# A decoder trunk on one core: memory values by token, projections moved between stages, and rotary queries with channels on partitions

## The chip, the cores and the metric

The kernel runs on one core of a Trainium2 chip. The metric is device time in microseconds (us) of one execution; lower is better. Engine names are those of the profile: PE is the matrix engine (PEld its weight loads), DVE the vector engine, ACT the scalar engine, POOL the general engine, SP the engine that issues every DMA here.

## The reference

Two layers (DEPTH) of a trunk with S = 1024 tokens and D = 1024 channels. Each layer projects the stream `x` into four token mixers of 4 heads each (MLA with a rotary part, stick-breaking, forgetting attention "fox", attention over 256 memory rows), gates each, merges the four with sigmoid gates and normalizes. What the change touches:

```python
def _rope(x, cos, sin):
    x1, x2 = jnp.split(x, 2, axis=-1)
    return jnp.concatenate([x1 * cos - x2 * sin, x1 * sin + x2 * cos], axis=-1)
...
    q = (_rms_norm(c_q, q_norm) @ w_qb).reshape(b, s, MLA_HEADS, MLA_NOPE + MLA_ROPE)
    q_nope, q_pe = q[..., :MLA_NOPE], q[..., MLA_NOPE:]
    q_pe = _rope(q_pe, cos[:, :, None, :], sin[:, :, None, :])
...
    mk, mv = jnp.split(mem @ w_mem_kv, 2, axis=-1)
    y_mem = _memory_attention(mem_q..., mk, mv)
```

All of it is float32. The kernel splits every operand into a high and a low part (fp32r) and forms a product in three matmuls: high by high, high by low, low by high (`passes`).

## The kernel before

The work of a layer is a chain of stages. A stage is a `run(units, filler, total)`: the attention units of one mixer (a unit is one head and one group of 256 queries, `qg`), and between their steps `total` steps of a filler, mostly projections (`proj`: 8 blocks of weights, two halves of 512 tokens, 16 steps of three 128x512 matmuls). The stages are fox pair 0, fox pair 1, stick-breaking ("sb") pair 0, sb pair 1, memory, then the preparation of MLA and the MLA units with the merge (`mg`) as filler. A scheduler of the framework fixes the order on each engine when the kernel is built; each engine then runs its list in order.

Weights come through `Stream`: `wload` fetches 128x512 blocks by an SP DMA, and POOL splits each into `wh` (L163) and `wl` (L166). All DMAs stand in one SP list, in which a DMA that waits holds up those behind it.

**Memory.** `mem_prep` forms keys and values of a pair of heads channel by token (`mk`, `mv`, 24 matmuls of 256 columns each); `v_from_T` copies `mv` out to `mvT` and turns it on PE (L328, two transposes a pair) to get values token by channel.

**Rotary queries.** `mla_qpe(half)` forms `qpeT` (128 channels, 512 tokens), copies it to `qT`, turns it token by channel with 4 transposes (L1007, tile `qpe`), applies the rotation on DVE (`rope`, six operations), scales on POOL (L1013) and writes high and low parts into `t4` tiles (`qt`). `mla_qpT(half)` turns these back with 16 transposes (L1028, tile `qpT`) into one operand `qpe` per head (copied by ACT, L1030). The third matmul of an MLA score (`sc<-kpe,qpe`, L378) reads it.

**MLA start.** The merge of branch 2 runs beside the preparation. `load_y(1)` fetches four gated outputs `y` of sb back from `y_d` (SP, L1044), and `split_y` splits them (`ybh` on ACT, L157; `ybl` on DVE, L158) for the merge of branch 1. Each unit also needs `s2` (two 64 KB DMAs, L355 and L356), its query tile with halves swapped. In sb, `tri`-masked tiles `bt` pass POOL's `affine_select` (L425), and PE turns them (L464) before the value products.

Of the kernel before, what the change touches and what calls it, by code (L numbers as in the profile page):

```python
# [65 lines left out]
def decoder_trunk(ctx: ExitStack, tc: tile.TileContext, x, x_t, mem_t, positions, w_a, w_s, mla_q_norm, mla_w_qb,  # L66
# [55 lines left out]
    def f(ap):  # L122
        return ap.bitcast(F32)
# [72 lines left out]
    c_d = dp.tile([4, S], F32, name="c_d")  # L196

# [29 lines left out]
    def wload(n):  # L227

        raw = rp.tile([P, HALF], F32, tag="wr", name=nm("wr"))
        i = nc.sync.dma_start(raw, w_s[n])  # L230
        if n < 4:
            after(i, last_load[0])
        wh = hp.tile([P, HALF], F32R, tag="wh", name=nm("wh"))
        wl = hp.tile([P, HALF], F32R, tag="wl", name=nm("wl"))
        split_pool(raw, wh, wl)
        return [(wh[:, c:c + P], wl[:, c:c + P]) for c in range(0, HALF, P)]
# [24 lines left out]
    class Stream:  # L261
# [11 lines left out]
        def take(self, n, ahead=8):  # L273
# [3 lines left out]
            return r  # L277
# [360 lines left out]

    for layer in range(DEPTH):
# [170 lines left out]
        def mem_prep():  # L810
            for pair in range(2):
                w = st.take(KT)
                ps = PJ("mk")
                yield from passes(ps[:, :MEM], w, memT, KT)
                a = U("mk")
                ks = (a[:, 0:MEM], a[:, MEM:])
                for t, r0 in zip(ks, (0, 64)):
                    act.copy(t[r0:r0 + 64, :], ps[r0:r0 + 64, :MEM])
                for t, r0 in zip(ks, (0, 64)):
                    lo = 64 - r0  # L820
                    dve.tensor_tensor(t[lo:lo + 64, :], ps[r0:r0 + 64, :MEM], f(t[r0:r0 + 64, :]), ALU.subtract)
                mo[pair]["k"] = ks
                w = st.take(KT)
                ps = PJ("mv")
                yield from passes(ps[:, :MEM], w, memT, KT)
                t = TMP("mvT")
                act.copy(t[:, :MEM], ps[:, :MEM])
                mo[pair]["v"] = v_from_T([t], 2)
                yield
# [25 lines left out]
        run(fox_units(fox[0], 0), pair_qkv(fox[1], SC64), 49)  # L855
# [6 lines left out]
        run(units(sb[0], "sb"), pair_qkv(sb[1], SC64), 49)  # L862
# [4 lines left out]
        run(units(sb[1], "sb"), chain(cq_proj(), proj(evac_mr)), 58)  # L867
# [3 lines left out]
        drain(mem_prep())  # L871
# [3 lines left out]
        run(units(mo[0], "mem") + units(mo[1], "mem"), chain(proj(stack_pair(mo[1]["q"], SC64)), gate(2, 0), gate(2, 1), gate(1, 0), gate(1, 1)), 80)  # L875
# [79 lines left out]
        t4s = [[], []]  # L955
# [24 lines left out]
        def load_wq():  # L980
            for k in range(3):
# [4 lines left out]
                for c0, c1, d0 in ((0, 64, 0), (64, 96, 256)):  # L986
                    n = 4 * (c1 - c0)
                    hv, lv = (t[:, d0:d0 + n].rearrange("p (h c) -> p h c", h=4) for t in (h, l))
                    split_pool(sv[:, :, c0:c1], hv, lv)
# [8 lines left out]

        def mla_qpe(half):
            ps = PJ("qpeT")  # L1000
            yield from passes(ps, wsl(wq_h, wq_l, 3, 256), cqT[half], 3)
            qT = U("qT", F32)
            act.copy(qT, ps)
            yield QPE_STEPS
            ps = PT("qpe")
            for b in range(4):
                pe.transpose(ps[:, b * P:(b + 1) * P], qT[:, b * P:(b + 1) * P], ident)  # L1007
            src = ps.rearrange("p (b h c) -> p b h c", b=4, h=4)
            qr = U("qr", F32).rearrange("p (b h c) -> p b h c", b=4, h=4)
# [107 lines left out]
        def step(f):  # L1117
# [3 lines left out]
        main = chain(mla_ckvT(), mla_k(0), mla_k(1), step(load_wq), step(lambda: load_cq(1)), mla_v(0), mla_v(1),  # L1121
                     split_cq(1), step(lambda: load_cq(0)), mla_qpe(1), split_cq(0), mla_q(1), mla_qpe(0), mla_qpT(1), mla_q(0), mla_qpT(0))
# [25 lines left out]
        run(units(ml[0], "mla") + units(ml[1], "mla"), mg, 96 - MG_EARLY - MG_LATE, False)  # L1148
# [145 lines left out]
```

## Time and profile before

| | |
|---|---|
| median of 3 runs | 1573.8 us (1573.46 to 1574.72) |
| profiled execution, its own time | 1577.04 us |
| its span, first to last instruction | 1575.3 us |
| mean granted PE clock | 0.997 of full |
| PE busy | 1554.1 us (99%) |
| DVE, ACT, POOL busy | 1041.6, 724.2, 779.2 us |
| moved by DMA | 127.92 MB, mean 81 GB/s |

A busy PE is not PE at its peak: a matmul's record runs until its end, and the next one starts well before that. What an instruction costs on a full PE is the distance between the starts of neighbours.

### The profile page before, as it was taken

Reading aid. Unit: us, or ns where it says so; the run is one execution under the profiler, and the core shown is the slowest. Engines: PE = TensorE matmul, PEld = TensorE weight load, DVE = VectorE, ACT = ScalarE, POOL = GpSimd, SP = SyncE. Lnnn points to the kernel's source line nnn. Section 1 sums busy time; section 2 is a strip of 40 time slices with the busy share of each in tenths; the row PEclk is TensorE's granted clock in tenths of the full one; section 3 lists DMA queues with packets and bytes.
Section 4 is the critical chain, followed back from the end, with each engine's and each line's share of the span. In section 5 each row is a group of like instructions: output and inputs, shape, how many; then the busy total and the mean of one; then the engine's idle time right before and its main releaser. Section 6 shows DMA issues by size and latency. Waiting matters only on the chain.

```text
span 1575.3 us, 24794 instructions
## 1 busy us (share of the span) xinstructions
PE 1554.1 (99%) x8454; PEld 1331.2 (85%) x8454; DVE 1041.6 (66%) x2055; ACT 724.2 (46%) x1612; POOL 779.2 (49%) x951
## 2 busy tenths in 40 slices
PE   9999999999999999999999999999999999999997
PEld 8888888888888888888898888888988887888886
DVE  7455699844436788973853566997454377888738
ACT  4354566534434656440323556565344346564400
POOL 5666525765544344671336655357655442446600
PEclk9999999999999999999999999999999999999999
DMA  5321112142233211252313211122312232212413
GB/s 185 115 71 41 47 41 64 54 125 64 74 109 109 70 55 44 81 176 72 124 63 100 65 45 45 37 69 73 111 54 90 96 111 64 65 33 87 152 52 116
DMA packets 86061, 127.92 MB, mean 81 GB/s; under 512 B 13424, under 2 KB 38832, under 8 KB 85936
## 3 DMA queue, kind: packets, MB, share of 16 engines
q1 hardware_dynamic: 85936, 126.34, 25.6%
q8 instruction: 67, 1.10, 0.3%
q14 instruction: 58, 0.48, 0.1%
HBM read 89.57 MB, written 19.96 MB: 70 GB/s over the span
## 4 chain that ended last, share of the span: by engine, by line
PE 90%; DVE 3%; POOL 2%; issue 2%; ACT 2%; DMA 1%; SPq 0%; DVEq 0%; POOLq 0%; ACTq 0%
PE pj L254 13%; PE pj L255 13%; PE pj L256 13%; PE y L494 7%; PE pt L464 6%; PE po L255 4%; PE po L256 4%; PE po L254 4%; PE sc L375 3%; PE sc L376 3%; PE pb L254 3%; PE pb L255 3%; PE pb L256 3%; PE pg L254 1%; PE pg L256 1%
## 5 line engine op out<-in xcount | busy, mean ns | idle before, releaser
L254 PE MATMUL pj<-xTh,wh 128*128 128x512 f32 x832 | 331.2, 398 | 2.2 <-DVE mx L433 1.4
L256 PE MATMUL pj<-xTh,wl 128*128 128x512 f32 x832 | 326.5, 392 | 0.0
L255 PE MATMUL pj<-xTl,wh 128*128 128x512 f32 x832 | 325.8, 392 | 0.0
L166 POOL TENSOR_TENSOR wl<-wr,wh 128x512 fp32r<-128x512 f32 x168 | 226.4, 1349 | 9.9
L155 DVE TENSOR_TENSOR pl<-pt,ph 128x384 fp32r<-128x384 f32 (+1 forms) x272 | 170.3, 638 | 69.9 <-ACT ph L154 68.3
L163 POOL TENSOR_SCALAR wh<-wr 128x512 fp32r<-128x512 f32 x168 | 117.0, 697 | 193.6 <-PE pj L255 113.4
L154 ACT CAST ph<-pt 128x384 fp32r<-128x384 f32 (+1 forms) x272 | 147.8, 550 | 138.4 <-PE pt L464 134.1
L256 PEld LDWEIGHTS pj<-xTh,wl 128*128 128x128 f32 x832 | 156.3, 188 | 31.7
L254 PEld LDWEIGHTS pj<-xTh,wh 128*128 128x128 f32 x832 | 156.5, 188 | 28.8 <-DVE mx L433 1.8
L255 PEld LDWEIGHTS pj<-xTl,wh 128*128 128x128 f32 x832 | 156.6, 188 | 25.5
L445 POOL TENSOR_SCALAR p<-p,sm 128x896 f32<-128x896 f32 (+7 forms) x128 | 102.3, 801 | 149.0 <-DVE sm L444 147.2
L134 ACT ACTIVATE p<-p,mx 128x896 f32<-128x896 f32 (+7 forms) x128 | 99.5, 777 | 67.3 <-DVE mx L433 60.5
L494 PE MATMUL y<-pl,v 128*128 128x256 f32 (+1 forms) x544 | 124.6, 306 | 0.0
L134 ACT ACTIVATE mg<-pg 128x512 f32<-128x512 f32 x128 | 76.0, 597 | 83.8 <-PE pg L256 41.9
L494 PE MATMUL y<-ph,v 128*128 128x256 f32 (+1 forms) x544 | 112.2, 283 | 1.8 <-ACT ph L154 1.6
L464 PE MATMUL pt<-ident_r,p 128*128 128x128 f32 x704 | 110.9, 273 | 0.2
L494 PEld LDWEIGHTS y<-ph,v 128*128 128x128 f32 x544 | 93.4, 189 | 13.8 <-ACT ph L154 1.8
L254 PE MATMUL pb<-ybh,wh 128*128 128x512 f32 x256 | 102.8, 401 | 0.9 <-DVE mg L1090 0.6
L438 DVE TENSOR_TENSOR_SCAN kt<-kt,unseen 128x896 f32<-128x896 f32 (+3 forms) x64 | 96.3, 1516 | 10.1 <-ACT kt L134 9.8
L255 PE MATMUL pb<-ybl,wh 128*128 128x512 f32 x256 | 100.6, 393 | 0.0
L256 PE MATMUL pb<-ybh,wl 128*128 128x512 f32 x256 | 100.4, 392 | 0.0
L464 PEld LDWEIGHTS pt<-ident_r,p 128*128 128x128 f32 x704 | 85.1, 140 | 13.8 <-issue 0.5
(273 smaller groups left out, 3555.9 us busy)
## 6 DMA issues: line engine op xcount, KB each, us to landing
wr<-in_w_s_dram SPq DMA_DIRECT2D x168, 256.0 KB, 2.6
s<-opA SPq DMA_DIRECT2D x128, 64.0 KB, 2.0
s<-opB SPq DMA_DIRECT2D x128, 64.0 KB, 2.0
wr<-in_w_out_dram SPq DMA_DIRECT2D x32, 256.0 KB, 2.7
xr<-in_x_t_dram SPq DMA_DIRECT2D x16, 256.0 KB, 5.3
ckb<-c_d SPq DMA_DIRECT2D x8, 512.0 KB, 3.9
y_d<-y SPq DMA_DIRECT2D x16, 256.0 KB, 2.0
y<-y_d SPq DMA_DIRECT2D x16, 256.0 KB, 3.6
```

Of the source, the lines that this page charges most:

```text
L134: i = act.activation(*args, **kw)
L154: act.copy(h, src)
L155: return dve.tensor_tensor(l, src, f(h), ALU.subtract)
L163: i = pool.tensor_scalar(h, src, 1.0, 1.0, ALU.mult, ALU.mult)
L166: pool.tensor_tensor(l, src, f(h), ALU.subtract)
L254: pe.matmul(ps, ah, bh, start=k == 0, stop=False)
L255: pe.matmul(ps, ah, bl, start=False, stop=False)
L256: pe.matmul(ps, al, bh, start=False, stop=k == nk - 1)
L438: dve.tensor_tensor_scan(kt[:, ::-1], kt[:, ::-1], unseen[:, S - w:][:, ::-1], 1.0, ALU.mult, ALU.max)
L445: pool.tensor_scalar(p, p, sm, 1.0, ALU.mult, ALU.mult)
L464: pe.transpose(pt[:, c:c + P], self.p[i][:, b * P:(b + 1) * P], ident)
L494: pe.matmul(u.y[:, q0 * P:256], u.op["v"][b][:, u.head, :], src[:, s * 256 + q0 * P:s * 256 + 256], start=j == 0 and n == 0, stop=j == n_c ...
```

## The change

**Memory.** The values are formed token by channel: the memory tokens are the stationary operand and 256 columns of weights the moving one (`take_two`), 48 matmuls of 256 columns as before, without `mvT` and its transposes. `mem_k(1)` moves into the filler of the memory stage.

**Moved projections.** The first of the three `cq` projections moves from sb pair 1 to sb pair 0 (total 49 to 65), `gate(2, 0)` from the memory stage into sb pair 1 (58 to 64); the memory stage goes from 80 to 72 steps. The weight blocks are put in the same order.

**Rotary queries.** In layer 0, `rotary_tables` turns cosine and sine once into tables with channels on partitions (16 transposes, beside fox pair 0) and stores them (`tab_d`, 4 DMAs of 256 KB). `load_tabs` fetches a 512 KB table for each half. `mla_qpe` now turns the queries where they stand: three DVE multiplies that read `qpeT` in PSUM and one DVE add, a copy of the high part on ACT, the low part on POOL. Four DMAs of 256 KB store the parts twice each (`qr_d`), and four of 256 KB fetch one operand `qpe` per head. `mla_qpT` is gone. `mla_q(0)` now stands ahead of `mla_qpe(0)`, and the second and third MLA units are swapped.

```diff
-            return r
+            return [(wh[:, c:c + P], wl[:, c:c + P]) for wh, wl, c in r]
+        def take_two(self):
+            self.pull(2)
+            (wh, wl, c), self.blocks = self.blocks[0], self.blocks[2:]
+            self.pull()
+            return wh[:, c:c + 2 * P], wl[:, c:c + 2 * P]
...
+    def rotary_tables():
+        for n, src in enumerate((cosT, sinT)):
+            for half in range(2):
+                rows = U("rows", F32)
+                pool.tensor_scalar(rows.rearrange("p (b r c) -> p b r c", b=4, r=8),
+                                   src[:, 4 * half:4 * half + 4, :].unsqueeze(2).broadcast_to((P, 4, 8, 16)), 1.0, 1.0, ALU.mult, ALU.mult)
+                ps = PT("tab")
+                for b in range(4):
+                    pe.transpose(ps[:, b * P:(b + 1) * P], rows[:, b * P:(b + 1) * P], ident)
+                t = TMP("tab")
+                if n == 0:
+                    act.activation(t, ps, AF.Copy, scale=SC96)
+                else:
+                    act.activation(t[0:64, :], ps[0:64, :], AF.Copy, scale=SC96)
+                    act.activation(t[64:128, :], ps[64:128, :], AF.Copy, scale=-SC96)
+                nc.sync.dma_start(tab_d[half][:, n, :], t)
+                yield
     for layer in range(DEPTH):
...
                 yield
             mem_raws.clear()
-        def mem_prep():
+        def mem_k(pair):
+            w = st.take(KT)
+            ps = PJ("mk")
+            yield from passes(ps[:, :MEM], w, memT, KT)
+            a = U("mk")
+            ks = (a[:, 0:MEM], a[:, MEM:])
+            for t, r0 in zip(ks, (0, 64)):
+                act.copy(t[r0:r0 + 64, :], ps[r0:r0 + 64, :MEM])
+            for t, r0 in zip(ks, (0, 64)):
+                lo = 64 - r0
+                dve.tensor_tensor(t[lo:lo + 64, :], ps[r0:r0 + 64, :MEM], f(t[r0:r0 + 64, :]), ALU.subtract)
+            mo[pair]["k"] = ks
+        def mem_v():
+            pss = [PJ("mv")[:, :256] for _ in range(2)]
+            for k in range(KT):
+                wh, wl = st.take_two()
+                for b in range(2):
+                    th, tl = (m[:, b * P:(b + 1) * P] for m in memT[k])
+                    pe.matmul(pss[b], th, wh, start=k == 0, stop=False)
+                    pe.matmul(pss[b], tl, wh, start=False, stop=False)
+                    pe.matmul(pss[b], th, wl, start=False, stop=k == KT - 1)
+                yield
             for pair in range(2):
-                w = st.take(KT)
-                ps = PJ("mk")
-                yield from passes(ps[:, :MEM], w, memT, KT)
-                a = U("mk")
-                ks = (a[:, 0:MEM], a[:, MEM:])
-                for t, r0 in zip(ks, (0, 64)):
-                    act.copy(t[r0:r0 + 64, :], ps[r0:r0 + 64, :MEM])
-                for t, r0 in zip(ks, (0, 64)):
-                    lo = 64 - r0
-                    dve.tensor_tensor(t[lo:lo + 64, :], ps[r0:r0 + 64, :MEM], f(t[r0:r0 + 64, :]), ALU.subtract)
-                mo[pair]["k"] = ks
-                w = st.take(KT)
-                ps = PJ("mv")
-                yield from passes(ps[:, :MEM], w, memT, KT)
-                t = TMP("mvT")
-                act.copy(t[:, :MEM], ps[:, :MEM])
-                mo[pair]["v"] = v_from_T([t], 2)
-                yield
+                mo[pair]["v"] = []
+            for ps in pss:
+                t = U("v").rearrange("p (h c) -> p h c", h=4)
+                src = ps.rearrange("p (h c) -> p h c", h=4)
+                act.copy(t[:, :, 0:64], src)
+                dve.tensor_tensor(t[:, :, 64:128], src, f(t[:, :, 0:64]), ALU.subtract)
+                for pair in range(2):
+                    mo[pair]["v"].append(t[:, 2 * pair:2 * pair + 2])
+            yield
         def gate_evac(n, pair):
...
         drain(pair_qkv(fox[0], SC64))
         fox[0].update(new_op())
         ys[(2, 0)] = fox[0]["y"]
-        run(fox_units(fox[0], 0), pair_qkv(fox[1], SC64), 49)
+        tables = () if layer else rotary_tables()
+        run(fox_units(fox[0], 0), chain(pair_qkv(fox[1], SC64), tables), 49 if layer else 53)
         fox[1].update(new_op())
         ys[(2, 1)] = fox[1]["y"]
         run(fox_units(fox[1], 1), pair_qkv(sb[0], SC64), 49)
         sb[0].update(new_op())
         ys[(1, 0)] = sb[0]["y"]
         table("sigmoid_and_others")
-        run(units(sb[0], "sb"), pair_qkv(sb[1], SC64), 49)
+        cqs = cq_proj()
+        run(units(sb[0], "sb"), chain(pair_qkv(sb[1], SC64), itertools.islice(cqs, 2 * KT)), 65)
         sb[1].update(new_op())
         ys[(1, 1)] = sb[1]["y"]
         for pair in range(2):
             mo[pair]["q"] = two_halves()
-        run(units(sb[1], "sb"), chain(cq_proj(), proj(evac_mr)), 58)
+        run(units(sb[1], "sb"), chain(cqs, proj(evac_mr), gate(2, 0)), 64)
         table("natural_log_exp_and_others")
         load_mem()
         drain(weave(proj(stack_pair(mo[0]["q"], SC64)), chain(split_mem(), cq_norm()), 1))
-        drain(mem_prep())
+        drain(mem_k(0))
+        drain(mem_v())
         table("exp_and_others")
         for pair in range(2):
             mo[pair].update(new_op())
-        run(units(mo[0], "mem") + units(mo[1], "mem"), chain(proj(stack_pair(mo[1]["q"], SC64)), gate(2, 0), gate(2, 1), gate(1, 0), gate(1, 1)), 80)
+        run(units(mo[0], "mem") + units(mo[1], "mem"), chain(proj(stack_pair(mo[1]["q"], SC64)), mem_k(1), gate(2, 1), gate(1, 0), gate(1, 1)), 72)
         for pair in range(2):
             ys[(3, pair)] = mo[pair]["y"]
         finish(chain(gate(0, 0), gate(0, 1)), 2)
...
                 yield from passes(ps, wsl(wq_h, wq_l, 3, pair * P), cqT[half], 3)
                 stack_pair(ml[pair]["q"], SC96, True)(ps, half)
+        tabs = {}
+        def load_tabs(half):
+            tabs[half] = K("tab").rearrange("p (a n) -> p a n", a=2)
+            nc.sync.dma_start(tabs[half], tab_d[half])
         def mla_qpe(half):
             ps = PJ("qpeT")
             yield from passes(ps, wsl(wq_h, wq_l, 3, 256), cqT[half], 3)
-            qT = U("qT", F32)
-            act.copy(qT, ps)
+            tab = tabs.pop(half)
+            rt = W("qr").rearrange("p (a n) -> p a n", a=2)
+            r, t = rt[:, 0], rt[:, 1]
+            dve.tensor_tensor(t[0:64, :], ps[64:128, :], tab[64:128, 1], ALU.mult)
+            dve.tensor_tensor(t[64:128, :], ps[0:64, :], tab[0:64, 1], ALU.mult)
+            dve.tensor_tensor(r, ps, tab[:, 0], ALU.mult)
             yield QPE_STEPS
-            ps = PT("qpe")
-            for b in range(4):
-                pe.transpose(ps[:, b * P:(b + 1) * P], qT[:, b * P:(b + 1) * P], ident)
-            src = ps.rearrange("p (b h c) -> p b h c", b=4, h=4)
-            qr = U("qr", F32).rearrange("p (b h c) -> p b h c", b=4, h=4)
-            qt = TMP("qt")[:, :256].rearrange("p (b h c) -> p b h c", b=4, h=4)
-            cs, sn = (t[:, 4 * half:4 * half + 4].unsqueeze(2).broadcast_to((P, 4, 4, 16)) for t in (cosT, sinT))
-            rope(qr, src, cs, sn, qt, dve.tensor_tensor)
-            pool.tensor_scalar(qr, qr, SC96, 1.0, ALU.mult, ALU.mult)
-            for b2 in range(2):
-                t4 = wp.tile([P, 2, 4, 4, ROPE], F32R, tag="W", name=nm("qt4"))
-                for b in range(2):
-                    t = t4[:, b]
-                    qb_ = qr[:, 2 * b2 + b].unsqueeze(2).broadcast_to((P, 4, 2, ROPE))
-                    act.copy(t[:, :, 0::2, :], qb_)
-                    dve.tensor_tensor(t[:, :, 1::2, :], qb_, f(t[:, :, 0::2, :]), ALU.subtract)
-                    t4s[half].append(t)
+            dve.tensor_tensor(r, r, t, ALU.add)
+            hl = wp.tile([P, 2, HALF], F32R, tag="W", name=nm("qrs"))
+            act.copy(hl[:, 0], r)
+            pool.tensor_tensor(hl[:, 1], r, f(hl[:, 0]), ALU.subtract)
+            for a in range(2):
+                for n in range(2):
+                    nc.sync.dma_start(f(qr_d[half, n, a]), f(hl[:, a]))
             yield
-        def mla_qpT(half):
-            for h in range(4):
-                pt = PT("qpT")
-                for b in range(4):
-                    pe.transpose(pt[:, b * P:(b + 1) * P].bitcast(F32R), t4s[half][b][:, h].rearrange("p a c -> p (a c)"), ident_r)
-                o = U("qpe")
-                act.copy(o, pt)
-                qpe[h][half] = o
-                yield
-            t4s[half].clear()
+            src = f(qr_d[half]).rearrange("r a (t h c) n -> h (r a t) c n", t=2, h=4)
+            for hd in range(4):
+                qpe[hd][half] = U("qpe")
+                nc.sync.dma_start(f(qpe[hd][half]), src[hd])
+            yield
         yb = {}
...
             f()
             yield
-        main = chain(mla_ckvT(), mla_k(0), mla_k(1), step(load_wq), step(lambda: load_cq(1)), mla_v(0), mla_v(1),
-                     split_cq(1), step(lambda: load_cq(0)), mla_qpe(1), split_cq(0), mla_q(1), mla_qpe(0), mla_qpT(1), mla_q(0), mla_qpT(0))
+        main = chain(mla_ckvT(), mla_k(0), mla_k(1), step(load_wq), step(lambda: load_cq(1)), step(lambda: load_tabs(1)), mla_v(0), mla_v(1),
+                     split_cq(1), step(lambda: load_cq(0)), step(lambda: load_tabs(0)), mla_qpe(1), split_cq(0), mla_q(1), mla_q(0), mla_qpe(0))
         def early():
             for _ in side:
...
         for pair in range(2):
             ml[pair].update(new_op())
         prep[0] = False
-        run(units(ml[0], "mla") + units(ml[1], "mla"), mg, 96 - MG_EARLY - MG_LATE, False)
+        mla = units(ml[0], "mla") + units(ml[1], "mla")
+        mla[1], mla[2] = mla[2], mla[1]
+        run(mla, mg, 96 - MG_EARLY - MG_LATE, False)
         finish(mg, 1)
         for pair in range(2):
             for half in range(2):
```

**What it does to the order.** SP where the MLA units begin, layer 0, before (`s` is the swapped query tile of a unit, `wr` a weight block, `y` the outputs of sb):

```order
L355 DMA s_1462_6281<-opA_6025 64x256
L356 DMA s_1462_6281<-opA_6025 64x256
L355 DMA s_1473_6315<-opA_6178 64x256
L356 DMA s_1473_6315<-opA_6178 64x256
L355 DMA s_1517_6448<-opB_6026 64x256
L356 DMA s_1517_6448<-opB_6026 64x256
L1044 DMA y_6330<-y_d 128x512
L1044 DMA y_6332<-y_d 128x512
L230 DMA wr_6913<-in_w_s_dram 128x512
L1044 DMA y_6334<-y_d 128x512
L1044 DMA y_6336<-y_d 128x512
```

SP at the same place now (`qrs` are the parts of the turned queries of half 0, `qpe` the operands of the four heads):

```order
L365 DMA s_1475_6309<-opA_6110 64x256
L1068 DMA qr_d<-qrs_6183 128x512 x2
L366 DMA s_1475_6309<-opA_6110 64x256
L1073 DMA qpe_6199<-qr_d 128x1x512
L1073 DMA qpe_6201<-qr_d 128x1x512
L1073 DMA qpe_6203<-qr_d 128x1x512
L1073 DMA qpe_6205<-qr_d 128x1x512
L1085 DMA y_6291<-y_d 128x512
L1085 DMA y_6293<-y_d 128x512
L1085 DMA y_6295<-y_d 128x512
L1085 DMA y_6297<-y_d 128x512
```

The four `y` loads now stand behind the four `qpe` loads, and these behind the stores of `qr_d`.

PE at the first MLA scores, layer 0, before (`sc` are scores, `qpT` the turned-back queries):

```order
L1028 MATMUL qpT_6142<-ident_r,qt_1373_5949 128x128 x2
L1028 MATMUL qpT_6142<-ident_r,qt_1374_5954 128x128 x2
L375 MATMUL sc_6246<-opA_5570,opA_6025 128x512
L376 MATMUL sc_6246<-opA_5570,s_1448_6237 128x512
L378 MATMUL sc_6246<-kpe_5542,qpe_6124 128x512
L1028 MATMUL qpT_6149<-ident_r,qt_1373_5949 128x128 x2
L1028 MATMUL qpT_6149<-ident_r,qt_1374_5954 128x128 x2
L1028 MATMUL qpT_6209<-ident_r,qt_1415_6109 128x128 x2
L1028 MATMUL qpT_6209<-ident_r,qt_1416_6114 128x128 x2
L375 MATMUL sc_6251<-opA_5607,opA_6025 128x384
```

PE at the same place now:

```order
L257 MATMUL pb_6190<-ybh_5438,wh_6012 128x512
L258 MATMUL pb_6190<-ybl_5439,wh_6012 128x512
L259 MATMUL pb_6190<-ybh_5438,wl_6013 128x512
L385 MATMUL sc_6216<-opA_5604,opA_6057 128x512
L386 MATMUL sc_6216<-opA_5604,s_1442_6207 128x512
L388 MATMUL sc_6216<-kpe_5576,qpe_5983 128x512
L385 MATMUL sc_6221<-opA_5641,opA_6057 128x384
L386 MATMUL sc_6221<-opA_5641,s_1442_6207 128x384
L388 MATMUL sc_6221<-kpe_5586,qpe_5983 128x384
```

The transposes between the scores are gone. From the last `qpeT` matmul of half 0 to the first score that reads `qpe_6199` there are now 60 PE instructions, 45 of them of 512 columns.

ACT at the first split of `y`, layer 0, now (`p` are softmax tiles, `ph` the high parts of turned tiles):

```order
L135 ACTIVATE p_6312,sm_6314<-p_6312,mx_6313 128x128
L135 ACTIVATE mg_6373<-pg_6369 128x512
L158 ACTIVATE ybh_6337<-y_6291 128x512
L158 ACTIVATE ybh_6341<-y_6295 128x512
L155 CAST ph_6380<-pt_6375 128x512
```

Before, the row `ybh` of the first `y` stood three rows ahead of a `ph`, and that of the second `y` right ahead of another; now both stand together ahead of one.

## Rows read from the trace of the kernel before

**Rows 1.** The page's first section: busy us of each engine, share, instructions.

```profile
PE 1554.1 (99%) x8454; PEld 1331.2 (85%) x8454; DVE 1041.6 (66%) x2055; ACT 724.2 (46%) x1612; POOL 779.2 (49%) x951
```

**Rows 2.** Busy us by stretch: both sb runs, memory, MLA units of layers 0 and 1.

```profile
core 0: us, PE busy (x) PEld busy (x) DVE busy (x) ACT busy (x) POOL busy (x), PEclk, DMA share, GB/s
197.00:325.00 128.00, 126.02 (x723) 109.31 (x721) 111.92 (x134) 75.38 (x168) 65.75 (x65) 1.00 0.20 61
...
350.00:440.00 90.00, 90.00 (x505) 77.60 (x504) 41.99 (x82) 40.03 (x113) 46.92 (x62) 1.00 0.23 71
...
525.00:550.00 25.00, 23.70 (x135) 19.98 (x136) 20.38 (x54) 19.18 (x42) 9.69 (x12) 1.00 0.33 96
...
1325.00:1350.00 25.00, 24.00 (x136) 21.00 (x137) 21.54 (x53) 16.19 (x36) 6.52 (x8) 0.93 0.12 37
```

**Rows 3.** Groups of instructions by line and shape: busy us, mean ns, idle before.

```profile
L1028 PE MATMUL qpT<-ident_r,qt 128*128 128x128 f32 x64 | 7.7, 243 | 1.2 <-ACT qpe L1030 1.2
...
L1007 PE MATMUL qpe<-ident_r,qT 128*128 128x128 f32 x16 | 2.4, 272 | 0.0
```

**Rows 4.** Timeline of PE, first MLA scores, layer 0: start, us, instruction.

```profile
522.62 0.79 PE L1028 MATMUL qpT<-ident_r,qt 128*128 128x128 f32 x8
523.25 0.47 PE L375 MATMUL sc<-opA,opA 128*128 128x512 f32 x1
...
524.02 0.81 PE L1028 MATMUL qpT<-ident_r,qt 128*128 128x128 f32 x8
524.97 0.44 PE L375 MATMUL sc<-opA,opA 128*128 128x384 f32 x1
```

**Rows 5.** Timeline of PE, the four transposes of one half.

```profile
516.27 0.60 PE L1007 MATMUL qpe<-ident_r,qT 128*128 128x128 f32 x4
516.62 0.30 PE L1028 MATMUL qpT<-ident_r,qt 128*128 128x128 f32 x1
```

**Rows 6.** Timeline of PE, ahead of a later group of transposes (idle in brackets).

```profile
527.12 0.39 PE L256 MATMUL pg<-mrh,wl 128*128 128x512 f32 x1
528.10 0.54 PE L1028 MATMUL qpT<-ident_r,qt 128*128 128x128 f32 x4 [0.59 <-ACT qpe L1030]
```

**Rows 7.** Timeline of PE in sb pair 0, layer 0.

```profile
220.37 0.28 PE L376 MATMUL sc<-opB,s 128*128 128x256 f32 x1
222.20 0.52 PE L464 MATMUL pt<-ident_r,bt 128*128 128x128 f32 x3 [1.54 <-POOL wh L163]
```

**Rows 8.** Timeline of ACT, a split of `y` in layer 0 and layer 1.

```profile
539.77 0.63 ACT L157 ACTIVATE ybh<-y 128x512 fp32r<-128x512 f32 x1 [1.11 <-DMA y<-y_d]
...
1324.50 0.63 ACT L157 ACTIVATE ybh<-y 128x512 fp32r<-128x512 f32 x1 [3.26 <-DMA y<-y_d]
```

**Rows 9.** Timeline of PE at these places, layer 0 and layer 1.

```profile
541.26 0.39 PE L494 MATMUL y<-ph,v 128*128 128x256 f32 x2
542.33 0.50 PE L375 MATMUL sc<-opA,opA 128*128 128x512 f32 x1 [0.68 <-DVE acc L1080]
...
1323.54 0.48 PE L494 MATMUL y<-pl,v 128*128 128x256 f32 x2
1325.65 0.51 PE L494 MATMUL y<-ph,v 128*128 128x256 f32 x2 [1.63 <-ACT ph L154]
...
1328.37 0.63 PE L254 MATMUL pb<-ybh,wh 128*128 128x512 f32 x1
```

**Rows 10.** DMA issues, us to landing: the page's row, and `y_d` both ways.

```profile
y_d<-y SPq DMA_DIRECT2D x16, 256.0 KB, 2.0
...
DMA to landing us min/median/max: 2.0/2.9/7.2
```

**Rows 11.** Timeline of SP, the last two of four `y` loads, layers 0 and 1.

```profile
534.93 0.79 SPq L1044 DMA_DIRECT2D y<-y_d  x2
...
1317.53 0.79 SPq L1044 DMA_DIRECT2D y<-y_d  x2
```

**Rows 12.** Durations of 128x512 instructions: DVE from PSUM, POOL, ACT (min/median/max ns).

```profile
L155 DVE TENSOR_TENSOR pl<-pt,ph 128x512 fp32r<-128x512 f32 x176 | 120.5, 686 | 59.2 <-ACT ph L154 58.1
...
L166 POOL TENSOR_TENSOR wl<-wr,wh 128x512 fp32r<-128x512 f32 x168 | 226.4, 1349 | 9.9
...
L1030 ACT CAST qpe<-qpT x16: 585/591/622, 518.9 to 1313.0; 128x512 fp32r<-128x512 f32 x16
```

More of the change, by code (lines that the diff above doesn't have):

```diff
@@ L1 @@
+import itertools
 from contextlib import ExitStack
@@ L196, in decoder_trunk @@
     c_d = dp.tile([4, S], F32, name="c_d")
+    tab_d = dp.tile([2, P, 2, HALF], F32, name="tab_d")
+    qr_d = dp.tile([2, 2, 2, P, HALF], F32R, name="qr_d")
     def rsqrt(dst, m, n):
@@ L235, in wload @@
         split_pool(raw, wh, wl)
-        return [(wh[:, c:c + P], wl[:, c:c + P]) for c in range(0, HALF, P)]
+        return [(wh, wl, c) for c in range(0, HALF, P)]
     def wload_o(src, k, col, tag, home):
@@ L954, in decoder_trunk @@
         cqT = [[], []]
-        t4s = [[], []]
         cq_raw = [[], []]
@@ L985, in load_wq @@
                 sv = raw[:, :384].rearrange("p (h c) -> p h c", h=4)
[L986 to L989, printed above, removed]
+                hv, lv = (t[:, :256].rearrange("p (h c) -> p h c", h=4) for t in (h, l))
+                split_pool(sv[:, :, 0:64], hv, lv)
+                hv, lv = (t[:, 256:384].rearrange("p (t h c) -> p t h c", t=2, h=4) for t in (h, l))
+                split_pool(sv[:, :, 64:96].rearrange("p h (t c) -> p t h c", t=2), hv, lv)
                 wq_h.append(h)
@@ L1250, in weight_blocks @@
             res += tile_of(w_in, base + 256 * i + pair * P)
-    for c0 in (0, P, 2 * P, MR0):
+    for c0 in (0, P, 2 * P, MR0, GZ0 + 2 * 256):
         res += tile_of(w_in, c0)
     res += tile_of(w_in, MQ0)
-    for c0 in (0, 256, P, 256 + P):
-        res += tile_of(w_mem, c0)
+    res += tile_of(w_mem, 0)
+    for k in range(KT):
+        res += [w_mem[k * P:(k + 1) * P, 256:256 + P], w_mem[k * P:(k + 1) * P, 256 + P:]]
     res += tile_of(w_in, MQ0 + P)
-    for n in (2, 1, 0, 3):
-        for pair in range(2):
-            res += tile_of(w_in, GZ0 + n * 256 + pair * P)
+    res += tile_of(w_mem, P)
+    for n, pair in ((2, 1), (1, 0), (1, 1), (0, 0), (0, 1), (3, 0), (3, 1)):
+        res += tile_of(w_in, GZ0 + n * 256 + pair * P)
     for n in (2, 1, 3, 0):
```

## Prediction

> **What bounds the kernel now.** I read the page's busy shares first. PE is busy 99% of the span, the next engine 66% [rows 1], so an instruction taken off PE shortens the kernel by what it occupies there, and one taken off another engine only where PE waits for it. I then read the stretches. In both sb runs together PE is busy 126.0 of 128 us and DVE 111.9; in the memory stage PE 90 of 90 and DVE 42; where the MLA units begin, PE misses 1.3 us of 25 in layer 0 and 1.0 in layer 1 while DVE works 20 to 21.5 [rows 2]. So there is little idle PE time to win anywhere, and most of what there is lies in sb and at the start of the MLA units. Last I read the timeline of PE at the places that the change touches, for two things: the distance between starts, which is what an instruction costs, and the waits.
>
> **PE work removed and added.** In both layers the change drops 64 transposes `qpT`, 16 `qpe` and 8 of `mvT` (4 a layer), and adds 16 for the tables, in layer 0 alone. The record of one lasts 243 or 272 ns [rows 3], but eight `qpT` start at 522.62 and the next matmul at 523.25, 0.079 us each [rows 4]; four `qpe` take 516.27 to 516.62, 0.088 each [rows 5]. `mvT` and the tables are the same shape and type as `qpe`, so I take 0.088 for them. 64 x 0.079 + 24 x 0.088 - 16 x 0.088 = 5.06 + 2.11 - 1.41 = **5.8 us saved**. The other bound goes by busy time, which is what was left of each record without overlap: 7.7 / 64 = 0.120 and 2.4 / 16 = 0.150 [rows 3], giving 7.7 + 8 x 0.150 = 8.9 us. I take the distances, since a neighbour starts there.
>
> A record of 272 ns read as cost would give 72 x 0.272 = 19.6 us. The Trainium skill, TensorE: Matmul & The Clock Gate, section PE-mode transpose, gives about 275 ns for one inside a kernel, which is the length of the record here; by that figure the sum would be 72 x 0.275 = 19.8 us. The distances speak against it, so it stands below as a rival only.
>
> Memory values by token are again 48 matmuls of 256 columns a layer, so they cost PE what the old ones did. The moved projections and `mem_k(1)` are the same instructions elsewhere: 22 filler steps a layer (16 and 6) more in sb, 8 fewer in the memory stage. Nothing for PE in the sum but the waits that they fill or open.
>
> **Waits removed.** Between the groups of `qpT`, PE stood for ACT to copy an operand out: at 524.02 eight transposes end at about 524.65 and the next matmul starts at 524.97, 0.32 us [rows 4]; the next group starts 0.98 us after a matmul of 512 columns where 0.23 to 0.26 is its due (three take 0.77 us from 523.25 to 524.02), 0.75 us [rows 4, 6]. About 1.05 us a layer, **2.1 us saved**, at least nothing if something else is late at that place.
>
> **sb.** In pair 0 PE stood 1.8 us from 220.37 to 222.20, ahead of the transposes of `bt`, 1.54 of them idle, put down to POOL [rows 7]. Layer 1 has the same wait. A filler step put in front would cover it, and 16 more steps come into this run. Since the order is made anew, the wait may also stay: bounds 0 and 2 x 1.7 = 3.4 us; I take about half, **1.8 us saved**. DVE is at 111.9 of 128 us here [rows 2]; the moved gate adds two DVE operations of 0.69 us a layer [rows 12], which the longer stage (22 steps of three matmuls, 22 x 0.77 = 17 us) covers.
>
> **The cost: rotary queries by DMA, and what stands behind them on SP.** A half goes through four DVE operations (0.69 us), a copy on ACT (0.59), a subtraction on POOL (1.35), stores that land after 2.0, and loads that land after 2.0 to 7.2, median 2.9 [rows 10, 12]. With four issues between at 0.4 us (two last 0.79) [rows 11], half 0 needs 2.75 + 0.6 + 1.35 + 1.6 + 2.0 + 2.9 = 11.2 us without a queue anywhere. The cover is the 60 PE instructions that the order puts between the last `qpeT` and the first score that reads `qpe_6199`: 45 of 512 columns at 0.77 for three, 11.6 us, and 15 narrower ones, about 1.5, so 13 us. Half 1 is formed some 90 PE instructions earlier and is safe. So half 0 arrives about 2 us early by this sum, and late as soon as DVE (three older operations of 0.69 stand ahead of it) or a store on SP is late.
>
> Next on SP come the four `y` loads. Before, the third was issued at about 534.9 and ACT stood until 539.77 for it; in layer 1 issue 1317.5, end of the wait 1324.50, ACT idle 3.26 us [rows 8, 11]. On PE this cost 0.68 us in layer 0, and in layer 1 1.63 us and then a lower clock: in 1325 to 1350 the granted clock is 0.93 on the mean, a matmul of 512 columns lasts 0.63 where 0.39 is usual, and 0.07 x 25 = 1.75 us of work is lost [rows 2, 6, 9]. Together 4.1 us that the old kernel already pays. Now 1 MB of `qpe` loads stands right ahead of the 1 MB of `y`, and two `ybh` stand together on ACT ahead of a `ph` that PE needs. One load occupied the DMA engines for about a quarter of the 4.8 us that four took, so `y` comes some 3 to 5 us later after its issue, and ACT, by an estimate from the order, reaches the first `ybh` about 4 us after that issue. I expect the sum of these waits to grow by 1 us a layer: **2.0 us lost**. Bounds: 4.1 us gained, if they vanish, and 7 us a layer lost (below).
>
> What else is added lies beside PE: the tables (four POOL and six ACT operations in fox pair 0 with POOL and ACT half idle [rows 1]), four stores of 256 KB there, and two 512 KB loads a layer issued a stage early. If a store of the tables held up SP, the query swap behind it would be late, one wait of 1 to 2 us once. DVE gets lighter in the preparation, with ten operations a half fewer and four more.
>
> **Sum.** -5.8 - 2.1 - 1.8 + 2.0 = -7.7 us. The profiled execution took 1577.0 us (span 1575.3 and 1.7 around it), 3.2 above the median, so 1569.3 by its own time and **1566 us** beside the median of 1573.8.
>
> **Rivals.**
> *A, slower: the SP queue binds.* The point is whether `y` or half 0 of `qpe` comes after PE has run out. For it: 2 MB in a row where 1 MB took 4.8 and 7.0 us (to the third landing), and the slowest load took 7.2 [rows 8, 10, 11]. Then `y` lands 10 to 14 us after the first `qpe` issue and ACT stands 4 to 7 us; PE, with some 2 us of work in hand, waits up to 5 us a layer and loses 1.75 more to the clock, about 7 a layer in place of nothing: -9.7 + 14 = +4.3, 1578 us. It eats the whole gain from 4.85 us a layer on. Against it: `y` took 4.8 us with other loads in between, and the first PE use of `y` stands some 40 PE instructions behind the matmuls that ACT evacuates right ahead of `ybh`.
> *B, the freed PE time becomes waits for DVE.* DVE works 20 of 25 us where the units begin [rows 2], and scores now follow each other without transposes between. Then the 3.5 us of transposes and 1.05 of waits a layer come back as waits, and only memory (0.7) and sb (1.8) stay: 1571.3. Against it: DVE has fewer operations just before.
> *C, transposes cost their record.* 19.6 + 1.9 of the rest: 1552. Against it, every distance in rows 4 and 5.
> *D, all these waits go.* -5.8 - 2.1 - 3.4 - 4.1 = -15.4: 1558.
>
> **How the numbers follow.** Forecast 0.53 (own range 1561.5 to 1570.5), A 0.17, B 0.13, C 0.04, D 0.13. This kernel can be told from no change beyond about 0.2%, 3.1 us: faster is below 1570.7, slower above 1576.9. Faster: the forecast nearly whole (0.49), D, C and a little of B (0.03): 0.69. Slower: over half of A, 0.10. Same: the rest, 0.21. The range 1557.5 to 1575.5 takes in D and B, and leaves out C and two thirds of A.
>
> **What would show it.** 72 fewer transposes on PE by count, and no `qpT` or `mvT`. PE's idle at L1028 gone. In sb pair 0 no idle above 1 us ahead of the transposes of `bt`; if it stays, that term is nothing. At the start of the MLA units: the wait of ACT ahead of `ybh` (1.1 and 3.3 us before), PE's wait ahead of the first `kpe,qpe` of the third unit, and the granted clock of that stretch. PE idle there above 5 us in a layer would be A; many waits of a few tenths for DVE would be B. A wait opened in the memory stage, now with 72 steps, or at the tables would make the sum wrong in a way that no term here holds.

## The result, and the profile after

The changed kernel takes 1576.1 us (median of 20 runs, 1574.0 to 1577.8), the kernel before 1573.9 (20 runs beside them); the ratio is 1.0013, interval 1.0008 to 1.0019. So the change costs about 2 us, where 7.7 were to be won. The profiled execution took 1576.1 us, span 1574.2.

The busy shares of the page answer to [rows 1]:

```profile
PE 1550.9 (99%) x8382; PEld 1325.5 (84%) x8382; DVE 1029.3 (65%) x2031; ACT 717.1 (46%) x1582; POOL 780.9 (50%) x955
```

There are 72 PE instructions fewer, as counted, and PE is as full as before. What was lost stands where the MLA units begin. Busy time by stretch of the changed kernel, with columns as in [rows 2]:

```profile
525.00:550.00 25.00, 20.77 (x101) 17.14 (x100) 13.66 (x40) 12.91 (x28) 8.62 (x11) 0.86 0.53 153
534.10:537.50 3.40, 3.40 (x13) 2.82 (x12) 1.36 (x3) 2.13 (x5) 0.37 (x1) 0.50 1.02 254
544.30:547.80 3.50, 3.50 (x14) 3.00 (x13) 3.47 (x9) 1.96 (x5) 0.48 (x1) 0.51 0.15 37
1300.00:1325.00 25.00, 19.70 (x102) 15.99 (x100) 14.66 (x37) 10.91 (x23) 9.23 (x10) 0.95 0.63 174
1325.00:1350.00 25.00, 24.95 (x137) 21.47 (x137) 20.87 (x56) 14.59 (x34) 8.28 (x10) 0.91 0.11 31
```

From 525 to 550 PE now misses 4.23 us (25 - 20.77) where it missed 1.30, and the granted clock is 0.86, another 0.14 x 25 = 3.5 us of work. In layer 1 it misses 5.30 and then 0.05 us, at 0.95 and 0.91: 1.25 and 2.25. That makes 16.6 us in both layers. The two narrow stretches show the clock at half, the lower of its two levels. The kernel before lost 1.30 there [rows 2], 1.00 and 0.07 x 25 = 1.75 from 1325 to 1350 [rows 2], and 1.75 in the stretch ahead of that, which this row of its busy time shows; 5.8 in all:

```profile
1300.00:1325.00 25.00, 23.25 (x133) 19.09 (x131) 15.31 (x44) 16.52 (x35) 9.02 (x11) 1.00 0.28 81
```

What PE waited for is in its timeline (idle and releaser in brackets):

```profile
531.18 0.39 PE L259 MATMUL pb<-ybh,wl 128*128 128x512 f32 x1
533.31 0.50 PE L388 MATMUL sc<-kpe,qpe 128*128 128x128 f32 x2 [1.74 <-DMA qpe<-qr_d]
...
534.92 0.63 PE L258 MATMUL pg<-mrl,wh 128*128 128x512 f32 x1
...
539.87 0.48 PE L504 MATMUL y<-pl,v 128*128 128x256 f32 x2
542.50 0.51 PE L504 MATMUL y<-ph,v 128*128 128x256 f32 x2 [2.14 <-ACT ph L155]
...
1314.47 0.50 PE L388 MATMUL sc<-kpe,qpe 128*128 128x128 f32 x2 [0.94 <-DMA qpe<-qr_d]
...
1324.29 0.80 PE L504 MATMUL y<-ph,v 128*128 128x256 f32 x2 [4.36 <-ACT ph L155]
```

First it waits for half 0 of `qpe`, then for ACT. ACT's own timeline tells why (it answers to [rows 8]):

```profile
540.07 0.63 ACT L158 ACTIVATE ybh<-y 128x512 fp32r<-128x512 f32 x1 [3.46 <-DMA y<-y_d]
541.34 0.63 ACT L158 ACTIVATE ybh<-y 128x512 fp32r<-128x512 f32 x1 [0.64 <-DMA y<-y_d]
541.88 0.57 ACT L155 CAST ph<-pt 128x512 fp32r<-128x512 f32 x1
...
1321.85 0.63 ACT L158 ACTIVATE ybh<-y 128x512 fp32r<-128x512 f32 x1 [4.57 <-DMA y<-y_d]
```

The `ph` that PE needs stands behind two `ybh`, and these stand for `y`. And `y` is late because of what SP does ahead of it. SP's timeline, and then the wait of its queue for the stores from 515 to 545 (us in total, times, longest):

```profile
523.15 0.81 SPq L1068 DMA_DIRECT2D qr_d<-qrs  x2
...
525.40 1.05 SPq L1068 DMA_DIRECT2D qr_d<-qrs  x2
526.50 0.47 SPq L366 DMA_DIRECT2D s<-opA  x1
529.32 2.53 SPq L1073 DMA_DIRECT2D qpe<-qr_d  x4
531.89 1.88 SPq L1085 DMA_DIRECT2D y<-y_d  x4
```

```profile
SPq L1073 <- DMA qr_d<-qrs: 2.2, 1, 2.2
```

The `qpe` loads of half 0 wait 2.2 us until the stores have landed (those of half 1, earlier, 3.6 us, with no `y` behind them). SP is one list, so the `y` loads stand behind that wait, and then 1 MB goes ahead of them: issued from 531.89, needed by ACT at 536.6 (540.07 - 3.46), there at 540.

The Trainium skill, DMA: Bandwidth & Descriptors, section Anatomy of one DMA — SWDGE (gpsimd) path, says that a semaphore wait is spent on the issuing sequencer ahead of dispatch, and that the DMA engines only work through their queues. The 2.2 us on SP agree.

sb kept its promise: from 221.63 to 223.48 PE goes through matmuls without a wait where it stood 1.54 us [rows 7], and in both sb runs of layer 0 nothing is missing where 1.98 us of 128 were [rows 2]:

```profile
197.00:325.00 128.00, 128.00 (x723) 109.86 (x722) 104.82 (x128) 72.09 (x163) 68.43 (x69) 1.00 0.21 63
```

### The profile page after: what moved, and what is told of

Same layout as the page of the kernel before. It is cut to its first block, busy times and chain, and to the rows that moved or that the text cites. A ratio compares the mean times of both kernels' runs of the same rounds, so it can differ in the third digit from the quotient of the medians.

```text
span 1574.2 us, 24644 instructions
## 1 busy us (share of the span) xinstructions
PE 1550.9 (99%) x8382; PEld 1325.5 (84%) x8382; DVE 1029.3 (65%) x2031; ACT 717.1 (46%) x1582; POOL 780.9 (50%) x955
## 4 chain that ended last, share of the span: by engine, by line
PE 93%; DMA 2%; DVE 1%; issue 1%; POOL 1%; SPq 1%; ACT 0%; DVEq 0%; POOLq 0%; ACTq 0%
PE pj L257 13%; PE pj L259 13%; PE pj L258 13%; PE y L504 7%; PE pt L474 7%; PE po L258 4%; PE po L257 4%; PE po L259 4%; PE sc L386 4%; PE sc L385 3%; PE pb L257 3%; PE pb L258 3%; PE pb L259 3%; PE pg L257 2%; PE pg L258 2%; PE pg L259 2%
## 5 line engine op out<-in xcount | busy, mean ns | idle before, releaser
L257 PE MATMUL pj<-xTh,wh 128*128 128x512 f32 x832 | 334.6, 402 | 2.3 <-DVE mx L443 1.4
L156 DVE TENSOR_TENSOR pl<-pt,ph 128x512 fp32r<-128x512 f32 (+1 forms) x272 | 171.6, 639 | 85.9 <-ACT ph L155 83.5
L167 POOL TENSOR_TENSOR wl<-wr,wh 128x512 fp32r<-128x512 f32 x168 | 221.4, 1319 | 10.2 <-PE pj L259 0.8
L155 ACT CAST ph<-pt 128x512 fp32r<-128x512 f32 (+1 forms) x272 | 147.2, 549 | 157.2 <-PE pt L474 152.3
```

The lines of the kernel that those rows point to most:

```text
L155: act.copy(h, src)
L156: return dve.tensor_tensor(l, src, f(h), ALU.subtract)
L167: pool.tensor_tensor(l, src, f(h), ALU.subtract)
L257: pe.matmul(ps, ah, bh, start=k == 0, stop=False)
```

## The experiments

Theory T1: the loss arises where the MLA units begin, from half 0 of `qpe` and the `y` loads behind it on SP (rival A of the prediction). T2: it arises elsewhere, in memory, the moved projections or the tables. Ratios are to the kernel before, with their 95% interval; its medians beside the three sets of four runs were 1573.7, 1574.1 and 1574.2. The scheduler makes the order anew for every kernel, so an edit can move more than its own lines. Some expectations give PE's waits 0.1 to 0.2 us longer than its timeline shows them.

| run | us | ratio |
|---|---|---|
| e1_rot_only | 1577.7 | 1.0026 (1.0016 to 1.0035) |
| e2_mem_only | 1571.9 | 0.9986 (0.9977 to 0.9994) |
| e3_y_early | 1570.4 | 0.9978 (0.9969 to 0.9988) |
| e4_qpe_early | 1585.5 | 1.0073 (1.0061 to 1.0086) |
| e5_y_earlier | 1564.6 | 0.9940 (0.9926 to 0.9954) |
| e6_pool_queue | 1570.0 | 0.9971 (0.9960 to 0.9982) |
| e7_y_earlier_pool_queue | 1568.1 | 0.9960 (0.9947 to 0.9973) |
| e8_units_not_swapped | 1573.5 | 0.9999 (0.9990 to 1.0008) |
| e9_old_rotary_y_earlier | 1570.4 | 0.9974 (0.9965 to 0.9983) |
| e10_sum_at_once | 1566.6 | 0.9952 (0.9940 to 0.9965) |
| e11_two_stores | 1566.8 | 0.9955 (0.9941 to 0.9968) |
| e12_old_rotary_swap | 1570.7 | 0.9980 (0.9971 to 0.9988) |

**The two halves of the change, apart (e1, e2).**

```diff
e1, against the changed kernel
-        run(units(sb[0], "sb"), chain(pair_qkv(sb[1], SC64), itertools.islice(cqs, 2 * KT)), 65)
+        run(units(sb[0], "sb"), pair_qkv(sb[1], SC64), 49)
...
-        drain(mem_k(0))
-        drain(mem_v())
+        drain(mem_prep())
e2, against the changed kernel
-                     ... mla_qpe(1), split_cq(0), mla_q(1), mla_q(0), mla_qpe(0))
+                     ... mla_qpe(1), split_cq(0), mla_q(1), mla_qpe(0), mla_qpT(1), mla_q(0), mla_qpT(0))
...
-        mla[1], mla[2] = mla[2], mla[1]
```

> The kernel before with the rotary part of the change alone (tables, rotary queries by DMA, order of the preparation, second and third MLA units swapped); memory and the moved projections as before. Theory T1 (the loss arises at the start of the MLA units, where half 0 of the rotary operand and then the y loads come late through the SP queue): this kernel is the slow part of the change, about 3 to 5 us over the kernel before (1577 to 1579), with PE waiting for qpe and for ph, and half-clock stretches there as in the changed kernel. Theory T2 (the loss arises elsewhere: in the memory stage, the moved projections or the tables): it is faster than before by about 4 to 6 us (the transposes and the waits between them gone), or within 1 us of it if the tables are to blame.

> The kernel before with the memory part alone (values by token, first cq projection into sb pair 0, one gate into sb pair 1, second key projection into the memory stage); rotary queries as before. T1: faster than before by 1 to 3 us (sb waits 2.5 and mvT transposes 0.7 saved, about 2 us given back in the memory stage). T2 with the memory stage to blame: slower than before by 2 us or more.

The rotary part alone costs 4.0 us, the memory part alone saves 1.8; together +2.2, which is what the whole change does. Both came as T1 said, so memory and the moved projections are not to blame. The tables belong to the rotary part, but they cost little: the first `mk` matmul of layer 0, behind them, starts at 330.0 in e1 against 328.8 before, and at 339.7 in the changed kernel against 338.2 in e2; that is 1.2 and 1.5 us, where the sum counted 1.41 (340.3 against 337.2, 3.1 us, between e5 and e9 below). T2 is out. In the timeline of PE of e1 the same two waits stand, and in the busy time by stretch of e2 the clock stays whole:

```profile
534.32 0.50 PE L388 MATMUL sc<-kpe,qpe 128*128 128x128 f32 x2 [1.14 <-DMA qpe<-qr_d]
544.09 0.80 PE L504 MATMUL y<-ph,v 128*128 128x256 f32 x2 [4.27 <-ACT ph L155]
...
1327.68 0.50 PE L504 MATMUL y<-ph,v 128*128 128x256 f32 x2 [3.15 <-ACT ph L155]
```

```profile
525.00:550.00 25.00, 23.16 (x130) 19.12 (x130) 19.29 (x53) 18.30 (x40) 9.68 (x12) 1.00 0.33 95
```

**The loads of `y` ahead (e3), the rotary operand ahead (e4).**

```diff
e3
-                if ct == KT - (1 if first else 2) and following is not None:
+                if ct == KT - (4 if first else 2) and following is not None:
                     load_y(following)
e4
-                     ... mla_qpe(1), split_cq(0), mla_q(1), mla_q(0), mla_qpe(0))
+                     ... mla_qpe(1), split_cq(0), mla_qpe(0), mla_q(1), mla_q(0))
```

> The changed kernel with the loads of y for the second merge issued three columns of the merge earlier, so that they stand on SP ahead of the stores and loads of half 0 of the rotary operand; nothing else moved by hand. T1: ACT's waits ahead of ybh (4.1 and 5.2 us) vanish, with them PE's waits of 2.3 and 4.5 us for ph and the half clock behind them (1.7 us for each of the later stretches); the wait of PE for qpe (1.9 and 1.1 us) stays. 1576 minus about 7 = 1567 to 1571. T2: within 1 us of the changed kernel, 1575 to 1577. A third reading (T3: the first wait, for qpe, pulls the rest with it): the wait for ph moves rather than goes, 1573 to 1576.

> The changed kernel with half 0 of the rotary queries formed ahead of both mla_q, so that its stores and loads stand ahead of the query swaps s2 of most MLA units on SP and have some 36 more matmuls of 512 columns (9 us) as cover. T1: PE's wait for qpe (1.9 and 1.1 us) and the first half-clock stretch go; the y loads then follow the query swaps, not the qpe loads, and are issued when their place in the order comes, so ACT's wait for y shrinks to the 1 to 3 us of the kernel before: 1568 to 1572. T2: 1575 to 1577. T3 (the wait for qpe pulls the rest with it): the whole gain, 1566 to 1569.

e3 fell by 5.7 us, as T1 wanted: no ACT wait for `y` is left. A new one came, here in PE's timeline: the 64 KB query swap `s` for the first unit, behind 1 MB of `qpe` (half 1) and 1 MB of `y`.

```profile
525.76 0.47 PE L386 MATMUL sc<-opA,s 128*128 128x512 f32 x1 [3.24 <-DMA s<-opA]
```

e4 went the other way, 9.4 us up, and T1's number for it was wrong. Its PE and SP timelines:

```profile
530.98 0.77 PE L386 MATMUL sc<-opA,s 128*128 128x512 f32 x1 [7.65 <-DMA s<-opA]
```

```profile
521.32 2.62 SPq L1073 DMA_DIRECT2D qpe<-qr_d  x4
523.99 0.52 SPq L366 DMA_DIRECT2D s<-opA  x1
524.56 1.22 SPq L365 DMA_DIRECT2D s<-opA  x2
```

With `mla_q` last, the queries are ready last and their swap has no cover; it is issued right behind the megabyte of `qpe` and is there 6.4 us after the issue of its second half (524.56 to 530.98). So here, as in the changed kernel, what stands last in the preparation pays for the megabyte.

**`y` further ahead, another queue, the old order of units (e5 to e8).**

```diff
e5
+                if ct == KT - (6 if first else 2) and following is not None:
e6 (e7: both)
-                    nc.sync.dma_start(f(qr_d[half, n, a]), f(hl[:, a]))
+                    nc.gpsimd.dma_start(f(qr_d[half, n, a]), f(hl[:, a]))
...
-                nc.sync.dma_start(f(qpe[hd][half]), src[hd])
+                nc.gpsimd.dma_start(f(qpe[hd][half]), src[hd])
e8
-        mla[1], mla[2] = mla[2], mla[1]
```

> The changed kernel with the loads of y issued five columns of the merge earlier (three in the run before this one), so that they stand on SP ahead of the loads of cq and of both halves of the rotary operand. In the run with three columns PE stood 3.24 and about 3 us for the query swap s behind 2 MB of qpe and y loads. T1 (too many bytes in front of s, qpe and y at one time): that wait goes too, and with it the half clock behind it: 1576 minus the 5.7 already found, minus 2 x 3 and about 1 to 3 of clock, 1561 to 1566. T4 (s is late because of the rotary loads alone): PE still waits 2 to 3 us a layer for s, 1569 to 1571.

> The changed kernel with the stores and loads of the rotary operand issued by POOL in place of SP; the same bytes, y and s stay on SP. If what costs is the order on SP (s, y and weights held behind a store that waits for POOL and a load that waits for the store): 1564 to 1570, with ACT's wait for y shorter than the 4.1 and 5.2 us of the changed kernel. If it is the bytes of the round trip (2 MB a half through the DMA engines): 1573 to 1577. If POOL pays for the issue, by more than SP did, its own work falls behind and PE waits for wl or p: above 1577.

> Both of the runs above at once: y five columns earlier, and the rotary operand by POOL's queue. If each takes away a wait of its own: lower than either by 1 us or more, 1559 to 1564. If both take away the same one: within 1 us of the better of the two.

> The changed kernel with the second and third MLA unit in their old order; nothing else. The second unit is then the first reader of half 0 of the rotary operand, some 20 PE instructions earlier. T1: PE's wait for qpe grows from 1.9 and 1.1 us to 5 or more a layer, and y is a little later too: 1580 to 1588. T2 (the loss arises elsewhere): within 1 us of the changed kernel.

e5 is the best kernel of all, 11.5 us under the changed kernel and 9.5 under the one before: `y` no longer meets `s` and `qpe`, and T1's number came. Its busy time by stretch, and the one wait for a DMA that is left in this stretch of PE's timeline:

```profile
525.00:550.00 25.00, 23.80 (x135) 19.98 (x134) 20.27 (x56) 16.60 (x35) 11.29 (x13) 1.00 0.39 127
1300.00:1325.00 25.00, 23.42 (x129) 19.50 (x130) 20.32 (x54) 16.34 (x34) 11.30 (x13) 1.00 0.40 127
```

```profile
535.64 0.50 PE L388 MATMUL sc<-kpe,qpe 128*128 128x128 f32 x2 [1.05 <-DMA qpe<-qr_d]
```

In e6 the same bytes move, those of the rotary operand from POOL's queue, and 6.1 us are won, at the edge of what was expected if the order on SP costs. So the bytes by themselves are not what costs. For `y` it is not SP's time either: its loads are issued 12.7 us after the start of the last `qpeT` matmul in layer 0 and 13.4 in layer 1, against 13.6 and 12.3 in the changed kernel. But they no longer stand behind the `qpe` loads in one list, and ACT has its first `ybh` of layer 0 without a wait. The new order also puts PE's first score of half 0 later, where PE does not wait for it (537.56, in the changed kernel 533.31). How the 6.1 us divide between the two is not shown. The rest of ACT's wait shows through on PE:

```profile
536.73 0.63 ACT L158 ACTIVATE ybh<-y 128x512 fp32r<-128x512 f32 x1
```

```profile
537.56 0.45 PE L388 MATMUL sc<-kpe,qpe 128*128 128x128 f32 x2
540.26 0.50 PE L504 MATMUL y<-ph,v 128*128 128x256 f32 x2 [0.59 <-ACT ph L155]
...
1318.50 0.50 PE L504 MATMUL y<-ph,v 128*128 128x256 f32 x2 [2.02 <-ACT ph L155]
```

The Trainium skill, DMA: Bandwidth & Descriptors, section Issuing engines are not separate DMA queues, says that starting DMAs from several engines saves only the sequencer's time to initiate them, usually small. Here 6.1 us were won with `y` issued no sooner; since the order on PE changed with it, this run alone does not speak against the page.

e7 missed both of its numbers. It is no better than e5 (0.9960 against 0.9940), so the two gains do not add up; most of what they remove is the same loss. Why it is 3.5 us worse stays open: from 525 to 550 PE is busy 24.02 us in it and 23.80 in e5.

e8 missed its number: undoing the swap made the changed kernel 2.5 us faster, not slower. In layer 0 PE has its first score of half 0 at about the same time (533.66 against 533.31), and ACT waits for `y` only 0.23 us; waits for POOL's `p` and for `qpe` came in its place, in PE's timeline:

```profile
529.69 0.44 PE L474 MATMUL pt<-ident_r,p 128*128 128x128 f32 x2 [1.29 <-POOL p L455]
530.79 1.54 PE L474 MATMUL pt<-ident_r,p 128*128 128x128 f32 x6 [0.66 <-POOL p L455]
533.66 0.79 PE L388 MATMUL sc<-kpe,qpe 128*128 128x128 f32 x2 [1.33 <-DMA qpe<-qr_d]
```

**Is the rotary part worth anything (e9, e12), and can the last wait go (e10, e11)?**

```diff
e9: e2 with e5's line and the unit swap; e12: e2 with the swap alone
e10: e5 with
-QPE_STEPS = 3
+QPE_STEPS = 1
e11: e10 with
-            for a in range(2):
-                for n in range(2):
-                    nc.sync.dma_start(f(qr_d[half, n, a]), f(hl[:, a]))
+            for n in range(2):
+                nc.sync.dma_start(f(qr_d[half, n]).rearrange("a p c -> p a c"), f(hl))
```

> The rotary queries as before (turned with tokens on partitions, no tables, no round trip), with the memory part, the second and third MLA unit swapped and the loads of y five columns earlier, as in the best run so far (1564.6), which differs from it by the rotary part alone. If the rotary part, freed of the y loads behind it, is worth what the prediction gave its PE work (5.1 us of transposes, 2.1 of waits, minus the 2 to 4 us that PE still waits for s and qpe in that run): 1567 to 1570. If early y loads are all the gain and the rotary part is worth nothing: 1564 to 1566. If it costs still: below 1564.

> The memory part alone (1571.9 in its own run) with the second and third MLA unit swapped, y loads where they were before. Undoing the swap made the changed kernel 2.5 us faster, with the rotary operand coming late. If the swap by itself costs (the order of the units): 1573 to 1575. If it cost there only because it put the y loads and the late qpe at one place: 1571 to 1573, no change.

> The run with y five columns earlier (1564.6), with the last DVE add of the rotation two steps of the side work sooner (QPE_STEPS 1 in place of 3); half 0 of qpe is then stored and loaded some 2 us sooner. If PE's waits of 1.26 and 1.09 us ahead of its first kpe,qpe of half 0 are due to that chain: they go, and the time falls by 1.5 to 3 us, 1561.5 to 1563. If the bytes in the queues set when qpe lands: no change, 1564 to 1565.

> The run above (y five columns earlier, the add sooner), with two stores of 512 KB a half in place of four of 256 KB: the same bytes, two issues on SP fewer, but the high part is stored only when POOL has formed the low part. If the issues on SP count: 0.5 to 1 us less than the run above; if only the bytes do: no difference (within 0.7 us).

e9 differs from e5 by the rotary part alone: 0.9974 against 0.9940, (0.9974 - 0.9940) x 1574 = 5.4 us, give or take 2.6 by the two intervals (by ratios, since the two ran in different sets). With `y` out of its way the rotary part gains that. e12 and e9 are alike within their intervals, so without the round trip early `y` is worth nothing that was measured, and the swap alone, e12 against e2, can't be told from nothing.

e10 was a miss, 2.0 us up where 1.5 to 3 down were expected (its interval and that of e5 overlap, so it may be no change), though PE's wait for `qpe` is gone. In PE's timeline others took its place:

```profile
527.21 0.44 PE L474 MATMUL pt<-ident_r,p 128*128 128x128 f32 x2 [0.55 <-POOL p L455]
529.38 0.50 PE L257 MATMUL pb<-ybh,wh 128*128 128x512 f32 x1 [0.90 <-DVE mx L443]
```

e11 is like e10: two issues fewer make no difference that was measured.

## Why the prediction was wrong

**The step that failed** is the term "I expect the sum of these waits to grow by 1 us a layer", 2.0 us. By the windows all waits and lower clock there, those removed at `qpT` counted too, grew from 5.8 to 16.6 us, by 10.8. In place of -2.1 + 2.0 this gives -5.8 - 1.8 + 10.8 = +3.2, where the medians say +2.2. (The two profiled executions say -0.9, that of before being the 3.2 us over its median that the prediction names; busy time by stretch is not exact enough to place these last few us.) Rival A had the mechanism and the place, at 0.17, and was priced at +4.3 where +2.2 came.

Two things went wrong in that term. First, its parts on `y` were nearly right, but the 1 us does not follow from them. `y` was put 3 to 5 us later than the 4.8 us after its issue, so 7.8 to 9.8, and came after 8.2 in layer 0 and 9.0 in layer 1; ACT was put at `ybh` 4 us after that issue and was there after 4.7 and 4.5. By these parts ACT stands some 4 to 6 us where it stood 1.1 and 3.3 [rows 8], and PE waits with it (2.14 and 4.36). Second, the wait for half 0 of `qpe` stood in no term. The round trip was put at 11.2 us "without a queue anywhere" against 13 us of cover. From the first DVE operation (519.18) to the score (533.31) it took 14.1: stores issued in two pairs up to 526.45, the first load 2.9 us later (529.32), then loads that stood behind nothing and still took 4.0. The growth also has no price for the clock, which only rival A has: 7.0 us of the 16.6 (3.5, 1.25 and 2.25) are lower clock behind such waits, against 1.75 before.

**Transposes, -5.8:** right by count and in size. e5 against e9 removes 64 of them on balance, 5.1 us at 0.079 each, and the waits for ACT ahead of `qpT` that e9 still has (0.58 and 0.56 us), and measures 5.4 with a wait for `qpe` left. The interval of 2.6 does not rule out the other bound of the prediction (7.7 for the `qpT`). Rival C is out: at their record of 243 ns the 64 would be 15.6 us. By the about 275 ns that the Trainium skill, TensorE: Matmul & The Clock Gate, section PE-mode transpose, gives for a bf16 one in a kernel, an estimate is 17.6; it is out too.

**Waits at `qpT`, -2.1:** gone with the instructions, and replaced by the longer ones.

**sb, -1.8, and memory, -0.7:** the wait went in both layers. In layer 1, from 980 to 1108, PE is busy 128.00 us where it was 126.00, so by busy time sb gives 4.0 us, over the upper bound of 3.4. e2 measures 1.8 (0.9 to 3.6) for the whole of this part. The memory stage gives some of it back with a wait for DVE that was not foreseen, 0.46 us at 371.48; where the rest goes is open. The count of steps in the text was off: the first `cq` projection only moves from one sb pair to the other, so sb as a whole gains the 16 steps of the gate, not 22. The memory run loses these 16 and gains the 8 of `mem_k(1)`, which stood ahead of it in the same stage.

**Rival B** (freed PE time comes back as waits for DVE) is out as the main cause, since e5 keeps the gain, but e10's waits are of that kind. **Rival D** did not come: even e5, with the waits for `y` gone, is 9.5 us under the kernel before, where D had 15.4.

## What to carry to other kernels

In this kernel a transfer that waited for another to land charged its wait (2.2 us), and its bytes (`y` came 8.2 us after its issue, 4.8 before), to the DMAs behind it in the list of the engine that issued it. Before replacing compute by a round trip through memory, list what stands behind it there (here `y` and `s`), give each its own cover, and move the loads that wait for nothing ahead of the round trip. A gain and such a loss can hide each other: here gains of 5.4 and 1.8 us and a larger loss made +2.2, and only the parts run apart, and each with the loads moved, showed both.

## What was not expected of the hardware

In layer 0 of the changed kernel the granted clock fell to its lower level behind PE waits of 1.74 and 2.14 us and stood at 0.50 and 0.51 for the 3.4 and 3.5 us shown above. In e8 it stood at 0.50 (530.80 to 534.50) behind waits of only 1.29 and 0.66 us close together. Waits of 0.94 (changed kernel, 1314), 1.05 (e5) and 1.14 us (e1) left it whole (1.00). A 64 KB transfer issued right behind 1 MB of loads was there only 6.4 us after its issue (e4).
